# LayerNorms that start inside the last MLP block, two token tiles at a time

## The chip, the cores and the metric

The kernel runs on one core of one Trainium2 chip. The metric is device time in microseconds (us) of one execution of the whole program; smaller is better. The kernel before takes 2342.94 us (median of three runs, 2338.77 to 2347.87).

## The reference

A decoder trunk of two layers works on 1024 tokens of width 1024, all in float32. Each layer is a mixer, a LayerNorm, an MLP and a second LayerNorm:

```python
for layer in range(DEPTH):                      # DEPTH = 2
    if layer % 2 == 0:
        mix = hybrid_mixer(x, ...)              # sliding-window attention + gated DeltaNet, output projection
    else:
        mix = recurrent_mixer(x, ...)           # convolution, RG-LRU scan, gelu gate, output projection
    x = layer_norm(DN_ALPHA * x + mix, ln1_g[layer], ln1_b[layer])
    x = layer_norm(DN_ALPHA * x + sqrelu_mlp(x, mlp_w1[layer], mlp_w2[layer]), ln2_g[layer], ln2_b[layer])

def sqrelu_mlp(x, w1, w2):                      # w1: 1024 x 4096, w2: 4096 x 1024
    h = jax.nn.relu(x @ w1)
    return (h * h) @ w2
```

`layer_norm` takes mean and variance over the 1024 features of a token, scales by `rsqrt(var + 1e-5)`, multiplies by a gain and adds a bias.

## The kernel before

**Two streams.** The tokens are cut into two chunks of 512, chunk 0 and chunk 1 (`c` in the code). `stream(c)` is a generator that walks one chunk through the layers: `hybrid`, `mix_out` (output projection, residual, LayerNorm), `mlp_ln` (MLP, LayerNorm), four `rec_block`s, `mix_out`, `mlp_ln`. Chunk 1 needs states of chunk 0 in the mixers, so it runs behind. Each product is made of three float32r matmuls (`mm3`): an operand is split into a rounded high part and the rest (`wh`, `wl` for weights, `h`, `l` for activations), and high by high, high by low and low by high are summed in PSUM.

**The order of the work.** A loop at the end of `trunk` pulls the two streams in turn. `yield` is a point at which other work may be slipped in, `yield UNIT` ends a unit of about 24 matmuls, and `yield BLOCK` says that a stream cannot go on. Which stream goes next is set by a sort key: not the one marked shy, then the lower phase, then chunk 0. A stream is marked shy after a unit in which its flag `light[c]` is set, so a light stream alternates with the other one, unit by unit. Beside the streams there are mixers, small generators put in by `spawn` (the LayerNorms among them); one goes as soon as the time it asked for has come in a clock that the planner keeps of all engines. TensorE executes its instructions in exactly the order that comes out. The instructions of VectorE (DVE), ScalarE (ACT), GpSimd (POOL) and the DMA queues are ordered by a scheduler under the data dependencies.

**Shared tiles.** `g` is a pool of 14 tiles of 128x2048, `t`, `s` and `f` are rings of 11, 10 and 4 tiles of 128x512 (`RINGS`). PSUM has four banks for long sums (`mm`) and four for short work (`mx`). A weight block of 128x1024 is loaded into `ws` by SP's queue, and `split` makes `wh` (ACT, every fifth on DVE) and `wl` (DVE, some on POOL).

**The MLP.** `mlp` cuts the 4096 hidden features into 8 blocks of 512. `straight(e)` computes block `e` in the plain way: 4 x 24 matmuls with w1, then 4 x 24 with w2. Two blocks can also be done as a pair `j`: `first(j)` computes 8 x 24 matmuls with w1, and `seven(j)` does the w2 product of the pair with seven products in place of eight (Strassen's form), each of 24 matmuls, with sums of w2 quarters (`t1` to `t4`) that DMAs have made in DRAM. In `seven` DVE forms the differences, makes every `wl`, splits the operands and adds each result to y. `weave` runs `first(j+1)` and `seven(j)` side by side; for the last pair, `seven(3)`, there is no `first` left. In the last MLP of chunk 1, block 6 is done straight, and the last block is held back (`ends`, `finish`) so that the tail is short. y of a chunk lies in two `g` tiles, each with two token tiles of 128 tokens (`ytile(yg, n)`, n = 0 to 3).

**The LayerNorm.** `layernorm` first loads gain and bias into four tiles of the ring that its argument `r` names (`load_gb`, on ACT's queue). `coef(a, b)` turns the statistics of token tiles a to b-1 into mean, scale and offset with a chain of small DVE instructions, `norm(n, i)` normalizes half `i` of tile `n` (one ACT and two DVE instructions, or two on DVE), and, where a next stage needs x, four TensorE transposes per half go to an `mx` bank, from which `split_ps` writes `yT` (the four `g` tiles of `ActT`). With `yT` None the halves are stored to `out` by SP's queue.

In the kernel before a LayerNorm is spawned when its sum is complete: by `mix_out` after `out_proj`, by `mlp_ln` after `mlp`. For chunk 0 in layer 0 it is spawned only when chunk 1 has used up its own input of the MLP (`"m7" in sts[1]`), and four `g` tiles are free. Only in the last MLP of chunk 1 does it begin with the first finished token tile.

## Time and profile before

| | |
|---|---|
| median of three runs | 2342.94 us |
| the profiled execution, its own time | 2344.71 us |
| span of its instructions | 2342.9 us |
| mean granted TensorE clock | 0.983 |
| TensorE (PE) busy | 2237.1 us, 95% |
| VectorE (DVE) busy | 1552.0 us, 66% |
| ScalarE (ACT) busy | 1026.9 us, 44% |
| GpSimd (POOL) busy | 313.0 us, 13% |

Busy time of PE counts overlapping matmuls once. A product of 128x512 is listed with some 0.39 us, and starts about 0.227 us after the one before it when nothing holds it up, so the rate of a stretch is read from the number of its matmuls and not from its busy share. Stages can be found in the trace by the DRAM tensors that SP loads: chunk 0's mixer ends at about 354 us, chunk 1's at about 826 us; chunk 0's first MLP ends at about 971 us, chunk 1's at about 1360 us; the recurrent blocks of both chunks run from 1268 to about 1603 us, and the last MLP of chunk 0 ends at about 2001 us.

### The profile page before, as it was taken

What the parts mean: (1) busy time and instruction counts of PE and PEld (TensorE: products, weight loads), DVE (VectorE), ACT (ScalarE), POOL (GpSimd) and SP (SyncE); (2) the same over time, 40 slices, a digit from 0 to 9 for tenths busy, and PEclk for the clock granted to TensorE, in tenths of its full rate; (3) what the DMA queues carried; (4) which work ended last, traced back from release to release, by engine and by line L of the source; (5) the groups of instructions that cost most, each with busy time, mean ns of one, the idle gap of its engine ahead of it and who ended that gap; (6) DMA issues with size and microseconds to landing.
All of it is one profiled execution on the core that took longest, in us unless ns stands there. A gap on an engine that the chain in (4) does not pass through costs nothing.

```text
span 2342.9 us, 31999 instructions
## 1 busy us (share of the span) xinstructions
PE 2237.1 (95%) x12460; PEld 1799.1 (77%) x12460; DVE 1552.0 (66%) x2631; ACT 1026.9 (44%) x1759; POOL 313.0 (13%) x245
## 2 busy tenths in 40 slices
PE   8999997999999999899999979999999999999997
PEld 7676775677777887788887858777788887788886
DVE  6788759565664565766567877776635567745677
ACT  5364415443433134444344657655234444343452
POOL 3332313223321120000000000000110000100000
PEclk9999999999999999999999989999999999999999
DMA  4220231556676755767643333433233443434452
GB/s 156 65 77 31 78 126 63 135 162 191 174 220 196 196 167 172 238 201 219 214 142 126 126 126 105 161 99 129 100 97 121 135 153 126 145 108 152 144 172 72
DMA packets 86199, 329.07 MB, mean 140 GB/s; under 512 B 9504, under 2 KB 9888, under 8 KB 77856
## 3 DMA queue, kind: packets, MB, share of 16 engines
q1 hardware_dynamic: 72944, 272.17, 34.2%
q0 software_dynamic: 4608, 33.56, 7.6%
q10 hardware_dynamic: 8496, 21.30, 2.6%
q8 instruction: 98, 1.61, 0.3%
q14 instruction: 53, 0.43, 0.1%
HBM read 318.60 MB, written 75.50 MB: 168 GB/s over the span
## 4 chain that ended last, share of the span: by engine, by line
PE 76%; DVE 15%; ACT 3%; issue 2%; DMA 1%; POOL 0%; ACTq 0%; DVEq 0%; POOLq 0%
PE mm L206 61%; PE mx L206 14%; DVE g L178 6%; DVE s L178 2%; DVE wl L178 2%; DVE t L178 1%; DVE hsc L178 1%; PE mx L210 1%; DVE f L178 1%; ACT wh L178 1%; DVE lnw L178 1%; ACT s L178 1%; ACT t L178 1%; DMA ws<-t 0%; DVE lns L178 0%
## 5 line engine op out<-in xcount | busy, mean ns | idle before, releaser
L206 PE MATMUL mm<-g,wh 128*128 128x512 f32 x2816 | 886.1, 396 | 4.3 <-DVE g L178 4.3
L178 DVE TENSOR_TENSOR wl<-ws,wh 128x1024 fp32r<-128x1024 f32 (+1 forms) x377 | 460.9, 1223 | 361.7 <-ACT wh L178 358.3
L178 ACT CAST wh<-ws 128x1024 fp32r<-128x1024 f32 (+1 forms) x350 | 364.9, 1043 | 718.8 <-PE mm L206 656.3
L206 PEld LDWEIGHTS mm<-g,wh 128*128 128x128 f32 x2816 | 521.3, 189 | 112.6 <-DVE g L178 5.9
L206 PE MATMUL mm<-g,wl 128*128 128x512 f32 x1408 | 550.4, 391 | 0.0
L206 PE MATMUL mm<-wh,s 128*128 128x512 f32 x1280 | 423.2, 398 | 13.3 <-DVE g L178 8.6
L206 PEld LDWEIGHTS mm<-g,wl 128*128 128x128 f32 x1408 | 265.3, 188 | 56.6
L206 PEld LDWEIGHTS mm<-wh,s 128*128 128x128 f32 x1280 | 242.8, 190 | 68.8 <-ACT wh L178 6.4
L206 PE MATMUL mm<-wl,s 128*128 128x512 f32 x640 | 251.7, 393 | 1.4 <-DVE wl L178 1.4
L178 POOL TENSOR_TENSOR wl<-ws,wh 128x1024 fp32r<-128x1024 f32 (+1 forms) x61 | 150.5, 2467 | 728.9 <-ACT wh L178 389.5
L206 PE MATMUL mm<-wh,g 128*128 128x512 f32 (+1 forms) x768 | 231.6, 379 | 9.7 <-ACT wh L178 6.8
L206 PE MATMUL mx<-wh,s 128*128 128x512 f32 x528 | 171.7, 392 | 1.8 <-DVE s L178 1.8
L206 PEld LDWEIGHTS mm<-wh,g 128*128 128x128 f32 x768 | 142.4, 191 | 36.3 <-ACT wh L178 6.8
L206 PE MATMUL mm<-wl,g 128*128 128x512 f32 (+1 forms) x384 | 143.9, 375 | 0.3 <-DVE wl L178 0.3
L206 PEld LDWEIGHTS mm<-wl,s 128*128 128x128 f32 x640 | 121.4, 190 | 25.2 <-DVE wl L178 1.8
L178 ACT CAST s<-g 128x512 fp32r<-128x512 f32 x158 | 95.5, 623 | 99.7 <-PE mx L206 47.4
L178 DVE TENSOR_TENSOR s<-g,s 128x512 fp32r<-128x512 f32 x158 | 105.9, 686 | 42.3 <-ACT s L178 42.0
L206 PEld LDWEIGHTS mx<-wh,s 128*128 128x128 f32 x528 | 99.1, 188 | 23.1 <-DVE s L178 3.1
L178 DVE CAST wh<-ws 128x1024 fp32r<-128x1024 f32 x88 | 60.5, 687 | 80.3 <-PE mm L206 70.3
L178 DVE TENSOR_TENSOR g<-g,mm 128x512 f32<-128x512 f32 x140 | 92.6, 683 | 27.9 <-PE mm L206 27.5
L206 PE MATMUL mx<-wl,s 128*128 128x512 f32 x264 | 102.8, 389 | 0.0
L206 PEld LDWEIGHTS mm<-wl,g 128*128 128x128 f32 x384 | 73.2, 191 | 12.2 <-DVE wl L178 0.6
(235 smaller groups left out, 2607.3 us busy)
## 6 DMA issues: line engine op xcount, KB each, us to landing
ws<-w SPq DMA_DIRECT2D x234, 512.0 KB, 3.3
ws<-t SPq DMA_DIRECT2D x88, 512.0 KB, 3.3
t<-w POOLq DMA_DIRECT2D x32, 1024.0 KB, 8.6
ws<-hin_fm SPq DMA_DIRECT2D x32, 512.0 KB, 3.4
t<-w SPq DMA_DIRECT2D x16, 1024.0 KB, 7.9
t<-t SPq DMA_DIRECT2D x16, 1024.0 KB, 7.4
ws<-rin SPq DMA_DIRECT2D x32, 512.0 KB, 3.3
ws<-hout SPq DMA_DIRECT2D x16, 512.0 KB, 3.4
```

What stands on the lines that cost most here:

```text
L178: r = f(*a, **k)
L206: ins = self.pe.matmul(out, lhsT, rhs, start=start, stop=stop, skip_group_check=fresh)
L210: return self._pe(self.pe.transpose(out, x, ident), out, [x], 0.00042 * 2 * out.shape[-1])
```

## The change

A LayerNorm is now spawned before its sum is complete. `out_proj` and `mlp` get a dictionary with a function `start` and a count `n` of finished token tiles; `start` is called ahead of the second half of the output projection, ahead of the last straight block, or ahead of the last `seven`. `layernorm` waits for `n` twice: it makes coefficients and begins to normalize when two token tiles are there, and again for the other two. It still waits for the tiles of `yT` before its first transpose.

The flag `light[c]` is set while `seven` runs with no `first` beside it. Chunk 1's LayerNorm after the first MLP takes its gain and bias tiles from ring `s` in place of `t`. In the last MLP of chunk 1 block 6, the straight one, moves from the start to the place ahead of the last `seven`.

```diff
@@ layernorm
-            coef(0, NT)
-            norm(0, 0)
             for j, (n, i) in enumerate(halves):
-                if j + 1 < len(halves):
+                if j % 4 == 0:
+                    yield from wait(lambda: res.get("n", NT) >= n + 2)
+                    coef(n, n + 2)
+                    norm(n, i)
+                if j % 4 < 3:
                     norm(*halves[j + 1])
+                yield from wait(lambda: yT.g)
                 yield late(2.5, ytile(yg, n)[:, i * 512:(i + 1) * 512])
@@ mlp, straight
                 if half == 1:
                     free(ring, *(z for hl in own for z in hl))
+                    if done:
+                        res["n"] = NT
@@ mlp, seven
+                    if done and i in (4, 6) and p == 1:
+                        res["n"] = 2 + (i == 6) * 2
                     yield UNIT
@@ mlp, body
-        if res is not None:
-            yield from straight(6, False)
         while e < 8 and not (...):
+            if e == 7:
+                res["start"]()
             yield from straight(e, e == 7)
             e += 1
         if e < 8:
-            n = 3 if res is not None else 4
+            n = 3 if tail else 4
             yield from first(e // 2)
             for j in range(e // 2, n):
-                nxt = first(j + 1) if j + 1 < n else ends() if res is not None else None
+                nxt = first(j + 1) if j + 1 < n else ends() if tail else None
+                if j == n - 1:
+                    if tail:
+                        yield from straight(6, False)
+                    else:
+                        res["start"]()
+                light[c] = nxt is None
                 yield from weave(nxt, seven(j, hids.pop(j), j == 3), 2)
-        if res is not None:
+                light[c] = False
+        if tail:
             yield from finish()
@@ out_proj
         for half in range(2):
+            if half == 1:
+                res["start"]()
...
                 oT.free()
+                res["n"] = NT
@@ mix_out
+        s["yT"] = ActT()
+        f = dict(n=0, start=lambda: spawn(layernorm(s["yg"], ls, which, r, s["yT"], f)))
+        yield from out_proj(w, oT, resid, s["yg"], ls, f)
...
-        spawn(layernorm(s["yg"], ls, which, r, s["yT"], f))
@@ mlp_ln
-        f = dict()
+        f = dict(n=0, start=lambda: spawn(layernorm(s["yg"], ls, 2 * layer + 1, r, s["x"], f, each)))
...
+        yield from mlp(layer, c, s["yT"], s["yg"], ls, f, last and c == 1)
+        if not last:
+            if c == 0:
+                yield from wait(lambda: "m7" in sts[1])
+            yield from need("g", 4)
+            s["x"].claim()
@@ stream
-        yield from mlp_ln(0, c, s, "t", False)
+        yield from mlp_ln(0, c, s, "ts"[c], False)
```

The program has the same 10868 matmuls and transposes as before, and the same number of ACT instructions and of DMAs. DVE has 75 instructions more: 78 more of the small ones of `coef` (each now twice, on 2 columns where it had 4), and three `wl` fewer, which go to POOL. Three places show how the order moves.

**Place 1: SP's queue at the end of chunk 0's first MLP.** SP loads the weight blocks in the order in which TensorE uses them. `w1_0` is the first MLP weight, here for chunk 1's `first(0)`; `t1_0_3`, `t2_0_3`, `t3_0_3` and `t4_0_3` are sums of w2 for chunk 0's `seven(3)`, and so is `w2_0`. Before:

```order
L178 DMA ws_1212_8601<-t1_0_3_117 128x1024
L178 DMA t4_1_1_128<-t2_1_1_127 128x2048
L178 DMA ws_1217_8623<-t1_0_3_117 128x1024
L178 DMA ws_1222_8648<-t2_0_3_119 128x1024
L178 DMA ws_1227_8670<-t2_0_3_119 128x1024
L178 DMA ws_1232_8696<-w2_0 128x1024
L178 DMA ws_1237_8718<-w2_0 128x1024
L178 DMA ws_1242_8745<-t3_0_3_118 128x1024
```

And now:

```order
L178 DMA ws_1213_8630<-w1_0 128x1024
L178 DMA ws_1221_8670<-t1_0_3_117 128x1024
L178 DMA ws_1224_8688<-w1_0 128x1024
L178 DMA t1_1_2_129<-w2_1 128x2048
L178 DMA ws_1230_8726<-t1_0_3_117 128x1024
L178 DMA ws_1233_8746<-w1_0 128x1024
L178 DMA ws_1239_8784<-t2_0_3_119 128x1024
L178 DMA ws_1242_8802<-w1_0 128x1024
```

Before, the products of `seven(3)` stood alone; now a w1 block (24 matmuls) stands between every two halves of a product (12 matmuls each).

**Place 2: TensorE at the end of chunk 1's first MLP.** `g_1043` and `g_1044` are the two y tiles of chunk 1, and `mx<-csb,g` are the transposes of the LayerNorm, four for each half of a token tile; the other rows are chunk 0's third recurrent block. Before:

```order
L206 MATMUL mx_1825_11903<-g_1621_10880,wh_1823_11899 128x512
L206 MATMUL mx_1825_11903<-g_1620_10879,wl_1824_11900 128x512
L210 MATMUL mx_1831_11964<-csb_75,g_1043_7515 128x128 x4
L210 MATMUL mx_1832_11974<-csb_75,g_1043_7515 128x128 x4
L210 MATMUL mx_1833_11985<-csb_75,g_1043_7515 128x128 x4
L210 MATMUL mx_1834_11995<-csb_75,g_1043_7515 128x128 x4
L210 MATMUL mx_1835_12006<-csb_75,g_1044_7516 128x128 x4
L210 MATMUL mx_1836_12016<-csb_75,g_1044_7516 128x128 x4
L206 MATMUL mx_1841_12034<-g_1618_10877,wh_1839_12030 128x512
```

And now, where `g_1044_7529` is the y tile of token tiles 2 and 3:

```order
L206 MATMUL mx_1830_11972<-g_1623_10933,wl_1829_11969 128x512
L210 MATMUL mx_1831_11976<-csb_75,g_1043_7528 128x128 x4
L210 MATMUL mx_1832_11986<-csb_75,g_1043_7528 128x128 x4
L206 MATMUL mx_1830_11972<-g_1623_10933,wh_1828_11968 128x512
...
L210 MATMUL mx_1833_12009<-csb_75,g_1043_7528 128x128 x4
L210 MATMUL mx_1834_12016<-csb_75,g_1043_7528 128x128 x4
...
L210 MATMUL mx_1875_12230<-csb_75,g_1044_7529 128x128 x4
```

Before, six groups of transposes stood in a row behind 24 matmuls of the block. Now the transposes of tiles 0 and 1 stand in two pairs among the first 24 matmuls after the MLP, and those of tiles 2 and 3 come 88 rows later (the first) to 157 rows later (the last).

**Place 3: SP's queue at the end of chunk 0's last MLP.** `w1_1` belongs to chunk 1's `first(0)` (before: to its `straight(6)`), the others to chunk 0's `seven(3)`; `out` are stores of chunk 0's result. Before:

```order
L178 DMA ws_2617_16447<-t4_1_3_136 128x1024
L178 DMA ws_2622_16469<-t4_1_3_136 128x1024
L178 DMA ws_2625_16491<-w1_1 128x1024
L178 DMA ws_2635_16607<-w1_1 128x1024
L178 DMA ws_2640_16643<-w1_1 128x1024
L178 DMA ws_2649_16683<-w2_1 128x1024
L178 DMA out<-g_1992_12845 128x512 x2
```

And now:

```order
L178 DMA ws_2638_16764<-w1_1 128x1024
L178 DMA ws_2644_16801<-t3_1_3_134 128x1024
L178 DMA ws_2651_16829<-w2_1 128x1024
L178 DMA ws_2656_16851<-t4_1_3_136 128x1024
L178 DMA ws_2661_16873<-w2_1 128x1024
L178 DMA out<-g_1932_12597 128x512 x2
L178 DMA ws_2666_16897<-t4_1_3_136 128x1024
```

Here too w1 blocks now stand between the products of `seven(3)`, and the first stores have moved ahead of its last weight block.

## The prediction

> **What bounds the kernel now.** I read the page first, then busy times by stretch, then the chain of waits and the instructions in order of time where TensorE stands still.

> ```profile
> PE 2237.1 (95%) x12460; PEld 1799.1 (77%) x12460; DVE 1552.0 (66%) x2631; ACT 1026.9 (44%) x1759; POOL 313.0 (13%) x245
> PE 76%; DVE 15%; ACT 3%; issue 2%; DMA 1%; POOL 0%; ACTq 0%; DVEq 0%; POOLq 0%
> ```

> TensorE is the bound, and 15% of the chain that ends last is DVE. The change leaves TensorE's instructions as they are, so it can only take away, or add, time in which TensorE waits. I need the rate when nothing holds it up. From the chain in order of time (start, length, engine, count), and from the instructions in order of time:

> ```profile
> 1020.57 16.32 PE mm L206 x72
> 913.89 1.04 PE L210 MATMUL mx<-csb,g 128*128 128x128 f32 x8
> ```

> 16.32/72 = 0.227 us for a 128x512 matmul and 1.04/8 = 0.13 us for a transpose. Now the stretches around the LayerNorms (bounds in us, length, then busy us and count of PE, PEld, DVE, ACT, POOL, then granted clock, DMA share and GB/s):

> ```profile
> 913.20:927.00 13.80, 12.75 (x70) 9.67 (x68) 12.74 (x18) 10.09 (x18) 1.19 (x1) 1.00 0.48 158
> 927.00:950.00 23.00, 22.41 (x99) 18.30 (x98) 22.77 (x29) 11.38 (x16) 0.35 (x1) 1.00 0.78 242
> 950.00:971.40 21.40, 15.42 (x59) 12.26 (x59) 13.07 (x19) 4.41 (x5) 0.46 (x1) 0.84 0.62 179
> 1015.00:1060.00 45.00, 45.00 (x200) 37.28 (x199) 29.44 (x35) 20.89 (x28) 0.82 (x1) 1.00 0.71 219
> ...
> 1268.10:1366.20 98.10, 95.83 (x422) 78.69 (x421) 81.74 (x110) 60.38 (x85) 7.96 (x14) 1.00 0.38 124
> 1371.60:1383.60 12.00, 0.18 (x1) 0.00 (x0) 8.64 (x23) 8.05 (x13) 0.00 (x0) 0.61 0.55 173
> 1383.60:1400.40 16.80, 13.38 (x57) 10.51 (x58) 13.32 (x23) 6.55 (x11) 0.00 (x0) 0.67 0.31 125
> 1400.40:1492.60 92.20, 89.32 (x385) 72.79 (x384) 71.71 (x95) 71.82 (x104) 9.03 (x12) 0.98 0.43 146
> ...
> 1536.20:1603.40 67.20, 62.40 (x274) 49.91 (x273) 56.97 (x96) 47.67 (x71) 4.71 (x3) 0.95 0.38 126
> ...
> 1955.60:2001.70 46.10, 39.85 (x158) 31.08 (x157) 39.84 (x71) 19.82 (x26) 2.88 (x1) 0.93 0.42 136
> 2041.10:2090.10 49.00, 49.00 (x218) 40.56 (x217) 16.50 (x18) 20.34 (x29) 0.00 (x0) 1.00 0.29 97
> ```

> A loss is the length less 0.227 us for each matmul and 0.13 us for each of the 32 transposes of a LayerNorm.
> - Place 1, chunk 0's first `seven(3)` with nothing beside it: 13.8 - 12.8, 23.0 - 22.4 and 21.4 - 13.4, together 9.6 us. From 927 to 950 DVE is busy for 22.77 of 23.0 us: `seven` alone feeds DVE as much as TensorE.
> - Place 2, chunk 1's LayerNorm after its first MLP: 12.0 with TensorE idle, 16.8 - (25 x 0.227 + 32 x 0.13 = 9.8) = 7.0, and 92.2 - 87.3 = 4.9, together 23.9 us. The 98.1 us before it, in which `seven(3)` and recurrent blocks alternate, lose 2.4.
> - Place 3, chunk 0's LayerNorm among chunk 1's recurrent blocks: 67.2 - (242 x 0.227 + 4.2 = 59.1) = 8.1 us.
> - Place 4, chunk 0's last `seven(3)`: 46.1 - 35.8 = 10.3 us.

> The stretch from 1015 us, where w1 blocks and `seven` alternate, loses nothing with DVE at 29.44 of 45.0 us; nor does the one from 2041, w1 blocks alone.

> What is late in place 1 and 2 stands in the chain of waits and in DVE's instructions (start, length; in brackets its idle time and what ended that):

> ```profile
> 949.93 10.58 DMA ws<-t
> 1376.21 4.70 DMA t<-ln
> ...
> 1368.66 0.69 DVE L178 BATCH_NORM_STATS2 lns<-g 128x6 f32<-128x512 f32 x1
> 1377.66 0.17 DVE L178 SCALAR_TENSOR_TENSOR lnw<-lnw 128x4 f32<-128x4 f32 x1
> 1380.93 0.75 DVE L178 SCALAR_TENSOR_TENSOR g<-g,lnw,t 128x512 f32<-128x512 f32 x1 [3.10 <-DMA t<-ln]
> 1383.52 6.11 DVE L178 TENSOR_TENSOR g<-g,t 128x512 f32<-128x512 f32 x10
> ```

> In place 2 the last statistics end at 1369.4, the coefficients at 1377.8 (their small instructions stand between others), and then DVE waits 3.1 us for gain and bias, which could not be loaded before ring `t` gave up tiles to chunk 0's recurrent blocks; the first transposes follow at 1383.6.

> **The change part by part.**

> *Gain and bias from ring `s`, an early start, two tiles at a time (place 2).* The load is out of the way, so at least the 3.1 us go. Token tiles 0 and 1 are complete after the fifth of seven products, and their coefficients and norms fall in the stretch from 1268 to 1366, where DVE has 16.4 us to spare; half a LayerNorm is 6 `TENSOR_TENSOR` and 2 `SCALAR_TENSOR_TENSOR` of some 0.7 us and a chain of 13 small ones of 0.17, about 8 us. That fits, barely, so I add 2 us of loss there. TensorE's order now holds the transposes of tiles 2 and 3 back by 88 to 157 rows, at least 88 x 0.227 = 20 us, against the 14 us from last statistics to first transposes now; without the hole the clock does not fall either. I keep 6 of 23.9 us, gain 18. Bounds: 3 (the load alone) and 22.

> The clock row bears on this: 0.61 granted in the hole, 0.67 in the 16.8 us behind it, where 7.0 us are lost with DVE busy for 13.32. [...]

> *`light` during the last `seven` (places 1 and 4).* The order shows 24 w1 matmuls between halves of 12: 36 x 0.227 = 8.2 us of TensorE, for which DVE makes two `wl`, one operand split, one addition to y and its share of differences. From the groups (busy us, mean ns, idle before):

> ```profile
> L178 DVE TENSOR_TENSOR wl<-ws,wh 128x1024 fp32r<-128x1024 f32 x15 | 18.3, 1218 | 8.2 <-ACT wh L178 8.1
> L178 DVE TENSOR_TENSOR s<-g,s 128x512 fp32r<-128x512 f32 x13 | 8.7, 682 | 0.3 <-ACT s L178 0.3
> L178 DVE TENSOR_TENSOR g<-g,mm 128x512 f32<-128x512 f32 x8 | 5.2, 681 | 0.0
> ```

> 2 x 1.22 + 0.68 + 0.68 + some 0.6 = 4.4 of 8.2 us, a share like that of the stretch from 1015. The 10.58 us load of place 1 then has w1 work ahead of it. The LayerNorm's transposes at 913 to 927 stay where they were (1.0 lost), and the last two products alternate with products of the other chunk's first `seven`, which DVE hardly keeps up with. I keep 1.6 of 9.6 and 2.3 of 10.3: gain 8 each. Bounds 0 and 9.6, 0 and 10.3; no row speaks for a loss, since only independent work comes in between.

> In place 4 the stores of token tile 0 stand in SP's queue ahead of the last weight block of `seven(3)`. Whatever is behind a late store waits. Tiles 0 and 1 are complete two products earlier, with w1 between them: 2 x 2 x 8.2 = 33 us less the alternating end, against 8 us of LayerNorm work. I count nothing; a late store would cost up to those 8.

> *The moved LayerNorm in place 3.* The spawn before the second half of `out_proj` brings only the load ahead, since both halves of the features are needed. The order puts this LayerNorm, as before, among recurrent blocks of chunk 1, where DVE is busy for 56.97 of 67.2 us; w1 blocks come later. Gain 2 of 8.1; bounds -5 (two more recurrent blocks are now behind it, at the 4.9 us that their stretch from 1400 lost) and 8.

> *Block 6 straight, later.* It is TensorE work with a light DVE load wherever it stands; the row from 2041 shows w1 work at no loss, and its place at the start of chunk 1's MLP is taken by `first(0)`, also w1. Zero; if it left a hole, one product's 5.4 us.

> *The first LayerNorm, among chunk 1's mixer.* Here the order is only reshuffled, with the transposes some rows earlier:

> ```profile
> 354.70:450.00 95.30, 80.90 (x707) 56.66 (x706) 75.12 (x196) 49.20 (x124) 26.45 (x20) 0.95 0.32 94
> 378.46 4.45 DVE L178 TENSOR_TENSOR g<-g,s 128x512 f32<-128x512 f32 x2
> ```

> TensorE stands idle for 14.4 us of it, and two norms took 4.45 us together, with POOL at work. Zero, from -8 to 8 (half of those 14.4 us either way, rounded up).

> *78 more small instructions.* At 0.17 us that is 13 us of DVE in six LayerNorms, which counts only where TensorE waits for DVE: in the first one and in places 2 and 3, three of six. Half of their 6.5 us fall between other instructions: 3 us lost; bounds 0 and 13.

> Sum: 18 + 8 + 8 + 2 + 0 - 3 = 33 us. The profiled execution took 2344.71 us, 1.8 above the median, so the changed kernel comes to 2311.7 in such an execution and to **2310 us** in the median.

> **The rivals.**
> - *DVE is late next.* With the load gone, norms and transposes of the second half wait behind recurrent work on DVE (81.74 of 98.1 busy before it, and it now takes 8 us more). Then place 2 gains 8, place 3 loses 1, places 1 and 4 gain 6 each: 8 - 1 + 12 - 3 = 16, 2327 us. For it speaks how full DVE is, against it the 88 rows. 13%.
> - *A shorter hole that still drops the clock.* If 4 of the 12 us remain in place 2, the 7.0 behind them stay as well, and the 4.9: the gain there is 8 in place of 18, 2320 us. 12%. [...]
> - *Loads hide the alternation.* At a DMA share of 0.78 a block took 10.58 us; the w1 blocks stand in the same queue, behind it. Places 1 and 4 gain 1 each: 33 - 14 = 19, 2324 us. Against it speaks the row from 1015, no loss at 0.71. 6%.
> - *Slower: DVE's queue in chunk 1's mixer.* The reshuffled first LayerNorm puts both coefficient chains and norms ahead of the attention and DeltaNet chains that TensorE waits for. One whole LayerNorm (16 us of DVE, two halves of 8) late at each of four heads is 64 us against 33: 2374 us. It decides from 45 us more of TensorE idle between 354 and 783. Only 14.4 of the first 95.3 us are idle there now. 4%.
> - *Not what it says:* the early start is held by `g` or ring tiles and nothing moves, 2343. The order of the engines shows it moving: 2%.

> **How the numbers follow.** My forecast has 63%, with its own range 2298 to 2321 (its unknown costs, most of them place 2 and the mixer). The range that holds 8 of 10 reaches to the second and third rival: 2298 to 2329. This measurement tells about 0.5% from no change, 11.7 us: faster means below 2331.2. All of the forecast, nearly all of the clock and load rivals and two thirds of the first lie there: 0.88. Within 0.5%: 0.08. Slower: 0.04.

> **What would show it.** Right: no TensorE idle of 10 us after chunk 1's first MLP, and a granted clock near 1.00 there; the two lone `seven(3)` run at 0.227 us per matmul. Wrong: DVE above 95% with TensorE waiting for `g` in place 2; waits for `wh` or for SP's queue in places 1 and 4; more idle time in chunk 1's mixer than now, above all.

## The result, and the profile after

The changed kernel takes 2314.1 us (median of four runs, 2311.93 to 2316.76) beside 2344.59 us for the kernel before; the ratio is 0.9873, with a 95% interval from 0.985 to 0.9896. Its profiled execution took 2313.61 us, with a span of 2311.8 us and a mean granted clock of 0.988. From the page of the changed kernel, the busy times and the chain of waits:

```profile
PE 2226.8 (96%) x12460; PEld 1795.1 (78%) x12460; DVE 1552.7 (67%) x2706; ACT 1026.1 (44%) x1759; POOL 313.6 (14%) x248
PE 78%; DVE 13%; ACT 3%; issue 2%; POOL 0%; DMA 0%; DVEq 0%; ACTq 0%; POOLq 0%
```

The program has 10866 matmuls and transposes, not 10868; the page counts 12460, 1594 more, and 1594 is the number of its f32 products that are not transposes: each of these stands there twice. DVE's part of the chain went from 15 to 13%, TensorE's from 76 to 78%. The stretches that answer to those of the prediction (bounds in us, length, then busy us and count of PE, PEld, DVE, ACT, POOL, then granted clock, DMA share and GB/s):

```profile
918.60:932.40 13.80, 12.75 (x70) 9.66 (x68) 12.75 (x18) 10.09 (x18) 0.00 (x0) 1.00 0.36 122
932.40:955.00 22.60, 22.01 (x98) 17.94 (x96) 16.39 (x20) 8.45 (x13) 0.81 (x1) 1.00 0.77 233
955.00:976.40 21.40, 21.40 (x96) 17.73 (x95) 11.88 (x13) 9.76 (x13) 0.81 (x1) 1.00 0.68 200
...
1361.70:1434.60 72.90, 69.66 (x321) 57.18 (x321) 66.13 (x105) 57.04 (x83) 8.62 (x13) 1.00 0.43 144
...
1478.20:1531.50 53.30, 45.01 (x201) 36.33 (x200) 47.46 (x95) 41.26 (x61) 5.40 (x3) 0.90 0.21 69
1934.60:1980.70 46.10, 45.51 (x201) 37.40 (x200) 27.32 (x32) 18.22 (x25) 0.00 (x0) 1.00 0.37 128
354.20:450.00 95.80, 82.69 (x677) 58.30 (x677) 69.93 (x189) 46.63 (x110) 28.02 (x21) 0.89 0.33 95
```

The first three rows are place 1, now with w1 blocks between: behind the LayerNorm's transposes TensorE is idle for 0.6 of 44.0 us, and DVE has fallen from 22.77 of 23.0 us to 16.39 of 22.6. The fourth is place 2. It keeps a granted clock of 1.00, where the kernel before had 0.61 and 0.67, and loses 72.9 us less 69.5 (the rate of the prediction), 3.4 us. The fifth is place 3 with a clock of 0.90 and 11.0 us lost, 8.3 of them idle. The sixth is place 4, now at its rate. The last is the start of chunk 1's mixer, where the clock is 0.89; before, the same stretch had 0.95.

At the ends of all the stretches below TensorE has done the same number of instructions in both kernels, and up to the end of E also the same work, so the time from one to the next can be compared directly. (At the end of F the changed kernel has done other blocks in part, since block 6 comes later there; they are matmuls of the same shape.) The four columns are start to start in us in four profiled executions: the first traces of the two kernels, and a second one of each from the runs below.

| stretch of TensorE's order | before | before, second | changed | changed, second |
|---|---|---|---|---|
| up to chunk 1's mixer | 347.9 | 347.0 | 347.9 | 346.3 |
| A: chunk 1's mixer, with the first LayerNorm | 558.5 | 558.4 | 564.4 | 564.3 |
| B: place 1 and chunk 1's first MLP | 335.7 | 329.8 | 327.6 | 327.6 |
| C: chunk 1's `seven(3)` with recurrent blocks | 117.3 | 117.3 | 115.6 | 115.6 |
| D: places 2 and 3 | 370.0 | 369.2 | 351.2 | 351.2 |
| E: chunk 0's last MLP up to place 4 | 201.3 | 201.3 | 201.3 | 201.3 |
| F: place 4 | 152.6 | 152.6 | 143.6 | 143.6 |
| G: the rest | 239.6 | 239.6 | 240.6 | 240.6 |

A row repeats within 1 us, apart from the first (1.6 us) and from B in the kernel before. The change takes 18 to 19 us out of D, 9.0 out of F, 1.7 out of C, and 2.2 or 8.1 out of B, and it puts 5.9 into A and 1.0 into G. Together the rows differ by 31 us in the first traces and by 25 in the second.

### The profile page after: what moved, and what is told of

Read it like the earlier page. It is cut to its first block, busy times and chain, and to the rows that moved or that the text cites. A ratio compares the mean times of both kernels' runs of the same rounds, so it can differ in the third digit from the quotient of the medians.

```text
span 2311.8 us, 32057 instructions
## 1 busy us (share of the span) xinstructions
PE 2226.8 (96%) x12460; PEld 1795.1 (78%) x12460; DVE 1552.7 (67%) x2706; ACT 1026.1 (44%) x1759; POOL 313.6 (14%) x248
## 4 chain that ended last, share of the span: by engine, by line
PE 78%; DVE 13%; ACT 3%; issue 2%; POOL 0%; DMA 0%; DVEq 0%; ACTq 0%; POOLq 0%
PE mm L206 61%; PE mx L206 16%; DVE g L178 5%; DVE t L178 2%; DVE s L178 2%; DVE hsc L178 2%; DVE wl L178 1%; PE mx L210 1%; DVE f L178 1%; ACT wh L178 1%; ACT g L178 1%; ACT t L178 1%; ACT s L178 1%; ACT f L178 0%; ACT L178 0%
## 5 line engine op out<-in xcount | busy, mean ns | idle before, releaser
L206 PE MATMUL mm<-g,wh 128*128 128x512 f32 x2816 | 890.1, 397 | 2.7 <-DVE g L178 2.6
L178 DVE TENSOR_TENSOR wl<-ws,wh 128x1024 fp32r<-128x1024 f32 (+1 forms) x374 | 456.8, 1222 | 340.0 <-ACT wh L178 336.7
L178 ACT CAST wh<-ws 128x1024 fp32r<-128x1024 f32 (+1 forms) x350 | 365.1, 1043 | 719.9 <-PE mm L206 620.6
L206 PEld LDWEIGHTS mm<-g,wh 128*128 128x128 f32 x2816 | 522.2, 189 | 111.3 <-DVE g L178 3.9
L206 PE MATMUL mm<-g,wl 128*128 128x512 f32 x1408 | 551.8, 392 | 0.0
L206 PE MATMUL mm<-wh,s 128*128 128x512 f32 x1152 | 379.8, 395 | 3.6 <-DVE g L178 3.3
L206 PEld LDWEIGHTS mm<-g,wl 128*128 128x128 f32 x1408 | 266.0, 189 | 57.0
L178 POOL TENSOR_TENSOR wl<-ws,wh 128x1024 fp32r<-128x1024 f32 (+1 forms) x64 | 157.2, 2457 | 1010.1 <-ACT wh L178 861.4
L206 PEld LDWEIGHTS mm<-wh,s 128*128 128x128 f32 x1152 | 216.2, 188 | 51.1 <-DVE g L178 3.9
L206 PE MATMUL mm<-wh,g 128*128 128x512 f32 (+1 forms) x768 | 231.4, 379 | 9.3 <-ACT wh L178 6.4
L206 PE MATMUL mm<-wl,s 128*128 128x512 f32 x576 | 224.6, 390 | 0.0
L206 PE MATMUL mx<-wh,s 128*128 128x512 f32 x528 | 172.7, 392 | 1.8 <-DVE s L178 1.8
L206 PEld LDWEIGHTS mm<-wh,g 128*128 128x128 f32 x768 | 142.3, 190 | 35.9 <-ACT wh L178 6.4
L206 PE MATMUL mm<-wl,g 128*128 128x512 f32 (+1 forms) x384 | 143.8, 375 | 0.3 <-DVE wl L178 0.3
L178 ACT CAST s<-g 128x512 fp32r<-128x512 f32 x158 | 96.4, 623 | 100.3 <-PE mm L206 51.2
L178 DVE TENSOR_TENSOR s<-g,s 128x512 fp32r<-128x512 f32 x158 | 106.8, 687 | 38.7 <-ACT s L178 38.5
L206 PEld LDWEIGHTS mm<-wl,s 128*128 128x128 f32 x576 | 108.3, 188 | 20.6 <-DVE wl L178 0.3
L206 PEld LDWEIGHTS mx<-wh,s 128*128 128x128 f32 x528 | 99.1, 188 | 23.2 <-DVE s L178 3.1
L178 DVE CAST wh<-ws 128x1024 fp32r<-128x1024 f32 x88 | 62.7, 712 | 78.1 <-PE mm L206 68.4
L178 DVE TENSOR_TENSOR g<-g,mm 128x512 f32<-128x512 f32 x144 | 95.0, 683 | 20.0 <-PE mm L206 19.5
L206 PE MATMUL mx<-wl,s 128*128 128x512 f32 x264 | 102.8, 389 | 0.0
L206 PEld LDWEIGHTS mm<-wl,g 128*128 128x128 f32 x384 | 73.2, 191 | 12.2 <-DVE wl L178 0.6
```

The source lines that it names most:

```text
L178: r = f(*a, **k)
L206: ins = self.pe.matmul(out, lhsT, rhs, start=start, stop=stop, skip_group_check=fresh)
```

## The experiments

The theory to begin with was the prediction's sum: terms that stand each for itself. So the first runs did single edits alone on the kernel before, or took single edits out of the changed kernel. Stretches are named by the letters above.

**`light` alone.** On the kernel before:

```diff
+                light[c] = nxt is None
                 yield from weave(nxt, seven(j, hids.pop(j), j == 3), 2)
+                light[c] = False
```

> The kernel before with one edit of the change alone: light is set during the last seven product, so that it alternates with w1 work. Theory A (the prediction's steps are separate terms): places 1 and 4 gain 8.1 and 8.9 us, everything else stays, 2344.7 - 17 = 2327.7 us in a profiled execution; the losses of about 9.6 and 10.3 us there fall to 1 to 2, and the 12.0 us hole of place 2 stays as it is. Rival B (the alternation needs the early LayerNorm to have something to alternate with, or is hidden behind the 10.58 us load): 2340 to 2345 us.

Measured: 2364.71 us, a ratio of 1.0116 (1.0098 to 1.0134), so slower by 27 us, which neither theory had. B took 330.0 us, like the second trace of before: nothing gained in place 1. F took 177.0 in place of 152.6. From the busy times by stretch of this run, and from ACT's instructions in order of time (start, length; in brackets its idle time and what ended that):

```profile
1966.00:2004.00 38.00, 28.43 (x96) 20.81 (x96) 16.31 (x20) 11.36 (x17) 2.39 (x1) 0.87 0.22 74
1969.20:1972.60 3.40, 3.40 (x9) 2.65 (x9) 0.00 (x0) 0.00 (x0) 0.00 (x0) 0.50 0.31 117
1982.90:1986.30 3.40, 3.40 (x9) 2.62 (x9) 2.64 (x3) 0.00 (x0) 0.00 (x0) 0.50 0.10 42
1996.50:1999.90 3.40, 3.40 (x9) 2.62 (x9) 0.00 (x0) 0.00 (x0) 0.00 (x0) 0.51 0.16 66
```

```profile
1973.12 1.06 ACT L178 CAST wh<-ws 128x1024 fp32r<-128x1024 f32 x1 [5.04 <-PE mx L206]
1978.38 1.04 ACT L178 CAST wh<-ws 128x1024 fp32r<-128x1024 f32 x1 [4.20 <-PE mm L206]
1979.33 0.59 ACT L178 ACTIVATE r<-mm 128x512 f32<-128x512 f32 x1
1979.95 0.63 ACT L178 ACTIVATE r<-r 128x512 f32<-128x512 f32 x1
1980.61 0.62 ACT L178 CAST s<-r 128x512 fp32r<-128x512 f32 x1
1981.13 0.61 ACT L178 CAST s<-g 128x512 fp32r<-128x512 f32 x1
```

In 38.0 us TensorE starts 96 matmuls, 21.8 us of work, with DVE busy for 16.31 us only. Of the 16.2 us lost TensorE is idle for 9.6. The rest is lost while it is busy, most of it in three stretches of 3.4 us behind the waits, with a granted clock of 0.50 to 0.51 and 9 matmuls in each, 2.0 us of work (over the 38.0 us the granted clock is 0.87). What is late is an operand. The half of a product that comes next needs `s<-g`, and ACT makes it as the last of a row: it waits for the w1 block of `straight(6)` to end (`r<-mm`), squares, converts that block's own operand (`s<-r`), and only then converts the one that TensorE waits for. That takes place at three w1 blocks in a row, each time with a wait of 2.5 to 3.3 us. ACT's queue of this kernel, in order (the operands of `seven(3)` are `s_16223` and `s_16288`):

```
L178 ACTIVATE r_16218<-mm_16193 128x512
L178 ACTIVATE r_16218<-r_16218 128x512
L178 CAST s_16179<-r_16218 128x512
L178 CAST s_16223<-g_15399 128x512
L178 CAST wh_16312<-ws_16310 128x1024
L178 ACTIVATE r_16280<-mm_16255 128x512
L178 ACTIVATE r_16280<-r_16280 128x512
L178 CAST s_16181<-r_16280 128x512
L178 CAST s_16288<-g_15399 128x512
```

In the changed kernel the same place reads so, with the operands of the two halves of `t1` (`s_16363`, `s_16418`) and the two before them one behind the other, well ahead of any wait for a w1 block:

```
L178 CAST s_16146<-g_15494 128x512
L178 CAST s_16227<-g_15493 128x512
L178 CAST g_16091<-mx_16139 128x4x128
L178 CAST s_16301<-g_15493 128x512
L178 CAST s_16363<-g_15493 128x512
L178 CAST s_16418<-g_15493 128x512
```

The code gives a reason: `straight` takes 8 tiles of one ring, with `s` first, and ring `s` has 10. `seven` also looks in `s` first and finds two, one pair, which cannot be filled again before its matmuls are done; `first` takes no ring tiles. Where the tiles lie in the built programs agrees. From the second half of `t1` to the end of `t4`, all nine half products of this kernel take their operands from one and the same pair of the ten places of ring `s`; in the kernel before they go round four pairs, in the changed kernel five.

The pair can be seen at work where nothing alternates any more. `straight(6)` cannot begin its w2 products while `seven` holds banks for long sums (`kept`), so behind the third w1 block the last four products of `seven(3)` stand alone, as in the kernel before. Yet they take 36.9 us here and 27.2 there, and each conversion starts only when TensorE is done with the half product before it:

```profile
2004.20 0.62 ACT L178 CAST s<-g 128x512 fp32r<-128x512 f32 x1 [3.34 <-PE mm L206]
2008.27 0.62 ACT L178 CAST s<-g 128x512 fp32r<-128x512 f32 x1 [2.50 <-PE mx L206]
```

**Block 6 at the start again.** On the changed kernel, to test this:

```diff
+        if tail:
+            yield from straight(6, False)
         while e < 8 and not (...):
...
                 if j == n - 1:
-                    if tail:
-                        yield from straight(6, False)
-                    else:
+                    if not tail:
                         res["start"]()
```

> The changed kernel with the six straight products of block 6 back at the start of chunk 1's last MLP. TensorE's order at chunk 0's last seven(3) is then that of the kernel before with light alone, which lost 24 us there. Theory A (formed after that run: block 6's w1 products write operands that hold 8 of the small ring's tiles until its w2 products, so seven has one pair of operand tiles and no look-ahead, and each half of 12 waits for ACT and DVE behind the w1 products beside it): place 4 takes 170 to 178 us in place of 143.6, about 2313.6 + 30 = 2344 us. Rival B (the prediction's: block 6 is light work wherever it stands, zero; what light alone lost came from the late LayerNorm there): 2312 to 2317 us.

Measured: 2346.98 us, a ratio of 1.0022 (1.0013 to 1.0032) to the kernel before. F, where TensorE's order is now that of `light` alone, took 179.3 us in place of 143.6 (a little above theory A's 170 to 178), all other stretches were those of the changed kernel within 1 us. Without the move of block 6 the whole change is worth nothing; with it, 34 us less (2312.94 in the same comparison). That block 6 beside `seven(3)` is what costs, once `light` makes the two alternate, is shown twice. That it does so through the tiles of ring `s` and ACT's queue is read from the programs and the trace above; no run changed the ring's size alone. The four cases of F (the lower row is from the changed kernel with and without `light`, the latter in the next run):

| F, us | without `light` | with `light` |
|---|---|---|
| block 6 at the start | 152.6 | 177.0 and 179.3 |
| block 6 ahead of the last `seven` | 146.5 | 143.6 |

**The changed kernel without `light`.**

```diff
-                light[c] = nxt is None
```

> The changed kernel without light during the last seven product. Theory A (separate terms): places 1 and 4 lose 8.1 and 8.9 us again, 2313.6 + 17 = 2330.6 us. Rival B (with the early start the last two products have nothing to gain from alternating, since the gain of places 1 and 4 came from the LayerNorm that begins under them): 2314 to 2318 us.

Measured: 2322.44 us, a ratio of 0.9937 (0.9923 to 0.9952). B took 332.8 and F 146.5 us. So `light` is worth 5.2 us (from one trace) and 2.9 us here, together 8.1 of the 17 us that theory A had. Of the 9.0 us that the change takes out of F, 6.1 come without it, with block 6 gone from there and the LayerNorm begun earlier. No run separates the two, but 5.3 us of loss are gone at one place, where the first w1 block of block 6 and a half product behind it stood; this speaks for block 6 (the place is shown further down, in the part on why the prediction was right).

**The kernel before, once more.** No edit.

> The kernel before once more, word for word. The kernel with the ring alone has the same work in place 1 and loses less there: 329.8 us from the w1 block to the next stretch, where the trace of before has 335.7. Theory A (the 10.58 us load of place 1 was late by chance in that one trace, and the change gains only some 2 us there): place 1 takes 329 to 331 us here, the other stretches are within 1 us of the first trace, profiled execution 2338 to 2341. Theory B (the load is late in every execution of before, and the ring moved it): 335 to 336, 2343 to 2346.

Measured: 2342.58 us, a ratio of 1.0002; the profiled execution took 2336.9 us and B 329.8. The prediction quoted a load of 10.58 us there, the third of three `ws<-t` blocks in a row. The same block in the first trace (issued at 949.93 us) and in this one (issued at 948.78), with its size and the time to landing:

```profile
ws<-t SPq DMA_DIRECT2D x1, 512.0 KB, 10.6
ws<-t SPq DMA_DIRECT2D x1, 512.0 KB, 6.0
```

And the last third of place 1, which had 59 matmuls in 21.4 us in the first trace:

```profile
948.80:970.20 21.40, 19.36 (x86) 15.73 (x85) 17.24 (x30) 5.92 (x7) 0.81 (x1) 1.00 0.80 244
```

The load takes 6.0 us and not 10.6, and place 1 loses 5.9 us less, as theory A had it. The late load belongs to an execution, not to the kernel. Of the 14 traces of this study one other, that of four tiles at once, has a load of over 10 us in place 1 (10.8 us). The executions of the kernel before lie between 2336.9 and 2349.1 us here, those of the changed one in its second comparison between 2312.3 and 2314.6.

**The ring alone.** On the kernel before:

```diff
-        yield from mlp_ln(0, c, s, "t", False)
+        yield from mlp_ln(0, c, s, "ts"[c], False)
```

> The kernel before with one edit alone: chunk 1's LayerNorm after its first MLP loads gain and bias through ring s in place of ring t. Theory A (as the prediction's lower bound: the load alone is worth the 3.1 us for which DVE waited, the coefficients and norms still come after the last statistics, so a hole of about 9 us and the slow clock behind it stay): 2341.6 us, gain 3. Rival B (the load was the whole of it: with it out of the way the other chunk's recurrent work fills the hole, the hole falls below 3 us and the clock does not drop): gain 15 to 18 in place 2, about 2328 us. Rival C (the hole shrinks to some 4 us and the 7.0 us of slow clock behind it stay): gain 8, 2337 us.

Measured: 2330.93 us, a ratio of 0.9965 (0.9953 to 0.9977). D took 359.7 us, 9.5 less than in the second trace of before. It is nearest to rival C. Place 2 in this run:

```profile
1366.00:1380.00 14.00, 9.33 (x35) 7.00 (x34) 13.79 (x27) 13.66 (x21) 0.00 (x0) 0.83 0.41 150
1371.80:1375.20 3.40, 1.43 (x6) 0.82 (x5) 3.37 (x6) 3.40 (x6) 0.00 (x0) 1.00 0.32 130
1375.20:1382.00 6.80, 5.64 (x15) 4.55 (x16) 6.80 (x13) 6.80 (x12) 0.00 (x0) 0.50 0.52 208
```

The hole of 12 us is now one of 1.5 and one of 3.1 us, both ahead of products of chunk 0's recurrent block, with DVE busy nearly all the time, and the clock still halves for 6.8 us behind them.

**Two tiles at a time, with ring `t`.** On the changed kernel, the ring edit taken back:

```diff
-        yield from mlp_ln(0, c, s, "ts"[c], False)
+        yield from mlp_ln(0, c, s, "t", False)
```

> The changed kernel with gain and bias of chunk 1's LayerNorm after its first MLP loaded through ring t again. Theory A (the early start needs the ring: ring t gives up tiles to chunk 0's recurrent blocks only behind them, so the LayerNorm cannot begin early and the 12 us hole with the slow clock behind it comes back): place 2 and 3 lose 12 to 20 us, 2326 to 2334 us. Rival B (two tiles at a time carries place 2, the planner finds room for ring t): within 4 us of the changed kernel, 2310 to 2318 us.

Measured: 2329.94 us, a ratio of 0.9945 (0.9928 to 0.9962), C 129.8 and D 353.2 us, together 16.2 us more than in the changed kernel. The size is theory A's, the place is not. The LayerNorm does begin early, but with four tiles of ring `t` in its hands, and chunk 0's recurrent blocks work in that ring: after three of their units of 24 matmuls TensorE's order has the last four products of `seven(3)` with nothing between, and then 24 transposes in a row. Around these transposes, busy times by stretch:

```profile
1306.00:1335.00 29.00, 16.13 (x68) 11.90 (x68) 25.43 (x62) 12.29 (x17) 0.00 (x0) 0.76 0.43 154
```

In ring `s` the load stands in nobody's way: TensorE has recurrent blocks between.

**All four tiles at once.** On the changed kernel, load and spawn as they are:

```diff
-                if j % 4 == 0:
-                    yield from wait(lambda: res.get("n", NT) >= n + 2)
-                    coef(n, n + 2)
+                if j == 0:
+                    yield from wait(lambda: res.get("n", NT) >= NT)
+                    coef(0, NT)
                     norm(n, i)
-                if j % 4 < 3:
+                if j + 1 < len(halves):
```

> The changed kernel, but each such LayerNorm begins its coefficients only when all four token tiles are complete, once for four tiles; load and ring stay as changed. Theory A (the two-tile early start carries most of the 18.7 us of place 2): place 2 loses 15 us more, chunk 1's mixer 3 us less with 78 small instructions fewer, 2313.6 + 12 = 2326 us. Rival B (the ring carries place 2, the two-tile step only adds small instructions): place 2 stays within 3 us, the stretch from 354 to 913 us is 3 to 6 us shorter, 2308 to 2311 us.

Measured: 2317.57 us, a ratio of 0.9916 (0.9901 to 0.993), between the two. D took 357.4 us, 6.2 more than the changed kernel; A took 559.9, 4.5 less. C and D together tell what carries place 2:

| kernel | C + D, us | gained |
|---|---|---|
| before, second trace | 486.5 | |
| the changed kernel with ring `t` | 483.0 | 3.5 |
| ring `s` alone | 477.0 | 9.5 |
| early spawn and ring `s`, four tiles at once | 473.0 | 13.5 |
| changed: ring `s`, two tiles | 466.8 | 19.7 |

3.5 (all of the change but the ring) and 9.5 (the ring) do not add up to 19.7: each edit makes room for the other.

**The changed kernel once more, and two kernels for stretch A.** The first has no edit. The second spawns the LayerNorms after the two `out_proj` at the old place; the third does that too and gives them four tiles at once.

```diff
-            if half == 1:
-                res["start"]()
...
         s["ln0"]["ln0"] = True
+        f["start"]()
```

```diff
+        m = NT if which % 2 == 0 else 2
...
-                if j % 4 == 0:
-                    yield from wait(lambda: res.get("n", NT) >= n + 2)
-                    coef(n, n + 2)
+                if j % (2 * m) == 0:
+                    yield from wait(lambda: res.get("n", NT) >= n + m)
+                    coef(n, n + m)
                     norm(n, i)
-                if j % 4 < 3:
+                if j % (2 * m) < 2 * m - 1:
```

> The changed kernel once more, word for word, so that its stretches stand beside those of the experiments on one chip. All theories: 2310 to 2317 us; place 1 (913 to 1249 us before) within 3 us of 327.6, chunk 1's mixer (354 to 913) within 2 of 564.4. If place 1 or the mixer differ by more, their differences between single traces are of that size too and a term that rests on one of them is no firmer.

> The changed kernel, but the LayerNorms after the two out_proj are spawned where they were before the change, after the claim of the tiles; two token tiles at a time stays. Theory A (what chunk 1's mixer lost, 5.9 us, comes from the early spawn, which puts load and norms at another place among its work): mixer 558 to 560 us, 2308 to 2310 us. Rival B (it comes from the second chain of 13 small instructions that DVE must do before the second half): mixer stays at 563 to 565, 2313 us.

> As the run before it, and those LayerNorms also take all four token tiles at once; only the LayerNorms after an MLP keep two at a time. Theory A (early spawn): nothing more than 1 us better than the run before it in chunk 1's mixer. Rival B (small instructions): mixer 558 to 560 us in place of 564, and place 3 (chunk 0's LayerNorm among recurrent blocks, 11.0 us lost) 2 to 3 us better, so about 2305 to 2308 us. Against both, the planner puts the transposes of place 3 one by one from 24 rows earlier on, which may give back some us there.

Measured: 2312.94 us for the changed kernel, a ratio of 0.988 (0.9863 to 0.9896); 2311.76 with the late spawn (0.9875, 0.9858 to 0.9891); 2314.45 with four tiles too (0.9882, 0.986 to 0.9903). A took 564.3, 564.0 and 561.9 us. So the early spawn costs A nothing, and the two steps of the first LayerNorm cost it some us. The third kernel gives that back in D, 355.0 in place of 351.2, where the planner has put the transposes of place 3 in other places.

**Four tiles for the first LayerNorm only.** So the next kernel keeps all of the change but for that one LayerNorm: the last diff without the late spawn, and with

```diff
+        m = NT if which == 0 else 2
```

> The changed kernel, but the first LayerNorm of each chunk takes all four token tiles at once; all others stay at two. TensorE's order after chunk 1's mixer is that of the changed kernel. Theory A (what the mixer lost is two holes that fill over half of a 3.41 us window each, at 363 and 394 us, in which the second coefficient chain stands in DVE's queue, so that the clock is halved for 3.4 and 10.2 us in place of once for 10.2): one slow stretch of 10.2 us is left between 354 and 450, the mixer takes 559 to 562 us in place of 564.4, 2309 to 2311 us. Rival B (the mixer's loss comes from the rest of the changed order): 564, 2313 us.

Measured: 2310.01 us (2305.53 to 2311.4), a ratio of 0.9856 (0.9838 to 0.9875). A took 558.9 us, as in the kernel before. What the two steps did to A, in busy times by stretch, first of the changed kernel and then of this one:

```profile
363.40:366.80 3.40, 1.47 (x8) 0.83 (x7) 3.40 (x21) 2.22 (x3) 0.67 (x3) 1.00 0.00 0
366.80:370.20 3.40, 3.40 (x11) 2.81 (x11) 3.40 (x10) 1.02 (x2) 0.00 (x0) 0.50 0.00 0
...
394.10:397.50 3.40, 1.30 (x10) 0.82 (x8) 3.30 (x6) 3.40 (x8) 1.30 (x2) 1.00 0.37 141
397.50:407.80 10.30, 8.22 (x51) 5.04 (x51) 7.18 (x14) 1.71 (x4) 4.34 (x3) 0.50 0.40 121
```

```profile
363.40:366.80 3.40, 2.50 (x19) 1.95 (x17) 3.40 (x15) 3.29 (x5) 0.00 (x0) 1.00 0.00 0
...
394.10:397.50 3.40, 2.83 (x47) 1.81 (x46) 3.26 (x6) 3.05 (x6) 1.63 (x2) 1.00 0.32 102
397.50:407.80 10.30, 8.64 (x85) 4.87 (x85) 8.47 (x18) 4.13 (x8) 3.05 (x3) 1.00 0.32 121
```

The holes themselves are short: in the first row TensorE is idle for 1.9 us of 3.4. But the clock halves behind them, for 3.4 and for 10.2 us; with one step the same stretches keep 1.00. Between 354 and 450 us the clock is halved for 20.5 us in the changed kernel, and for 10.2 in this one and in the kernel before. This kernel has the lowest median of the study, but its interval overlaps that of the changed kernel (0.9863 to 0.9896), so it is not shown to be faster; in the traces the spans are 2308.5 beside 2311.8 and 2310.4 us. What is shown is the direction in A. TensorE's order in A is the same in all kernels with two steps there, and with one step it is that of the kernel before. The six traces with two steps have A at 563.4 to 564.5 us, the eight with one step at 556.7 to 562.2.

**And `light` during the second `out_proj`.** On that kernel, in `stream`:

```diff
-        light[c] = False
         yield from mix_out(I["rout"], ...)
+        light[c] = False
```

> As the run before it, and light stays set for chunk 0 during its second out_proj, so that it alternates with recurrent blocks of chunk 1 and the LayerNorm of place 3 begins later among other blocks. Theory A (place 3 loses 11.0 us because DVE is full there, and more TensorE work ahead of its transposes fills part of the 5.9 and 2.6 us holes): place 3 gains 3 to 6 us, 2305 to 2308 us. Rival B (DVE has the same work for the same TensorE work, so the hole only moves): within 2 us of the run before it. Rival C (its transposes stand singly between products now, and each waits): 2 to 5 us slower than the run before it.

Measured: 2310.83 us (0.986, 0.984 to 0.988). D took 353.5 beside 351.5 us: the holes of place 3 moved and did not go (rival B). A took 562.2 us beside 558.9, though TensorE's order there is the same; the last section tells why.

## Why the prediction was right, and where it was not

**The sum.** 33 us were forecast and 2310 us; it came to 28 to 30 us by the ratios, 2313 to 2314 us. The time is within the likeliest case's own range. The terms are less good than their sum, and that the sum came near is in part luck, as the terms of place 4 and block 6 show.

**Place 2, gain 18.** Its loss fell from 23.9 to 3.4 us, and the 2 us of loss that I added for the stretch before it were a gain of 1.7 (C). The step held: no idle of 10 us is left, the clock stays at 1.00, and DVE is full (66.13 of 72.9 us) but makes TensorE wait for 2.0 us only. My lower bound, 3 us for the load alone, was too low: the ring alone gave 9.5, because gain and bias in time let the planner move the transposes too.

**`light` in places 1 and 4, gain 8 each.** This is the step that failed, in its size and in its ground. In place 1 I sized the loss from one execution with a late load; the second trace has 5.9 us less, and the gain left is 2.2 us. (I also put that load beside a DMA share of 0.78; it was issued at 949.93 us, and the row in which it ran has 0.62.) In place 4 the 9.0 us came, but only 2.9 of them by `light`. And "no row speaks for a loss, since only independent work comes in between" is wrong. The work was independent, but ACT's queue and the ring were shared, and `light` alone cost 24 us in F. A row of the kernel before already spoke for it. There one w1 block of block 6 stands between two halves of a product, from 1955.60 us, and the half behind it waits for its operand:

```profile
1964.48 0.57 PE L206 MATMUL mm<-wh,s 128*128 128x512 f32 x1 [3.28 <-ACT s L178]
```

The block and the half lose 5.3 us together, half of the 10.3 us of place 4, which the prediction treated like place 1, as time lost to DVE. (What it says of a late store in SP's queue is in that trace too: a store that had waited 4.2 us for DVE goes out at 2007.40 us and takes 0.34, and the weight load behind it follows at 2007.84, without a wait of its own.) `light` on the kernel before made three more such places. In the changed kernel without `light` the w1 block there is one of `first(0)`, and neither it nor the half behind it loses anything.

**Block 6, zero.** Wrong by 34 us in the changed kernel, where `light` is set. I looked at what block 6 does to DVE and at w1 work at no loss in the row from 2041, but that work is `first`, which takes no operand tiles. The two wrong steps cancel in the changed kernel, since there block 6 is out of the way when `light` sets in. In place 4 the gain came out near the forecast for a reason that the prediction did not have.

**Place 3, gain 2.** It lost 2.9 us more, 11.0 in place of 8.1, within the bounds. DVE is at 47.46 of 53.3 us, and the holes are at its norms; TensorE's instructions in order of time:

```profile
1512.17 1.11 PE L210 MATMUL mx<-csb,g 128*128 128x128 f32 x4 [5.69 <-DVE g L178]
1515.53 1.22 PE L206 MATMUL mx<-s,wh 128*128 128x512 f32 x2 [2.24 <-DVE g L178]
```

**The first LayerNorm 0, small instructions 3.** Stretch A lost 5.9 us more, within the bounds of -8 to 8. The two steps were the right thing to cost, the price was not that of the instructions, 0.17 us each. It was what the clock does behind the short holes that come with the two steps: one step for that LayerNorm gave back 5.5 us in that trace, and between 1.2 and 7.8 us over all traces with one and with two. Whether the second chain itself or the order that comes with it makes the holes was not separated.

**The rivals.** The slower one, in chunk 1's mixer, named a place that did lose, at a tenth of its price; 45 us of idle time were far off. A shorter hole that still drops the clock did not come in place 2, but it is what the ring alone shows there, with holes of 1.5 and 3.1 us and 6.8 us at half clock, and what A shows, with 1.9 us of idle time and 3.4 us at half clock. The 4 us that this rival left of the hole were an assumption. The case that would have made the change worthless, two streams whose operands share a queue and a ring, was not among the rivals.

## What to carry to other kernels

Work that is independent on the engine that sets the end can still meet in the queue of a helper engine and in the tiles of a ring, as `light` alone showed here at a price of 24 us: before two streams are made to alternate, look at which operands each holds and at the order of the conversions on the other engine's queue, and cost each edit with and without the others. Take a stall's size from more than one execution when a transfer ends it: the same load took 10.6 us in one and 6.0 in another. And count a small hole by what the clock does behind it, not by its own length: 1.9 us of idle time at 363 us had 3.4 us at half clock behind them.

## What was not expected of the hardware

| the window began at | busy share of it | before: windows, and followed by the other clock | changed | 14 traces |
|---|---|---|---|---|
| full clock | less than 45% | 7, 7 | 6, 6 | 105, 101 |
| full clock | 45 to 62% | 7, 3 | 6, 1 | 93, 18 |
| full clock | more | 643, 0 | 643, 0 | 9021, 0 |
| half clock | at least 80% | 12, 10 | 8, 7 | 127, 119 |
| half clock | less | 9, 0 | 6, 0 | 71, 0 |

The bounds of 45, 62 and 80% only sort these counts; no run shows where a limit lies. Not all windows that were followed by half clock were idle: 1.9 us of idle time did it at 363 us (a window 43% busy), while the hole of 1.84 us in place 2 of the changed kernel, of which 1.6 us lie in one window, 54% busy, did not:

```profile
1366.90:1370.30 3.40, 1.82 (x10) 1.61 (x11) 3.40 (x9) 2.26 (x4) 0.00 (x0) 1.00 0.51 154
1370.30:1373.70 3.40, 3.40 (x16) 2.79 (x16) 3.40 (x7) 1.06 (x1) 0.10 (x1) 1.00 0.00 0
```

The raster does not follow the program: the last two kernels have the same order on TensorE in stretch A and the same hole of 2.43 us near 485 us. In the one without `light` in `out_proj` the raster cuts the hole in two windows, 61 and 68% busy, and nothing follows:

```profile
482.80:486.20 3.40, 2.07 (x11) 1.46 (x10) 3.40 (x2) 1.04 (x1) 3.40 (x3) 1.00 0.00 0
486.20:489.60 3.40, 2.30 (x10) 1.93 (x11) 3.40 (x8) 0.40 (x2) 0.69 (x1) 1.00 0.79 219
```

In the other it lies in one window, 29% busy, and the next 3.4 us run at half clock:

```profile
484.30:487.70 3.40, 0.97 (x5) 0.49 (x4) 3.40 (x3) 1.04 (x1) 2.76 (x2) 1.00 0.15 28
487.70:491.10 3.40, 3.40 (x9) 2.63 (x9) 3.34 (x8) 0.40 (x2) 0.00 (x0) 0.50 1.06 273
```

With a second such pair, near 420 us, this makes A 3.3 us longer in the one execution than in the other. Differences of that size between single executions of kernels with holes of 2 us tell nothing about the kernels. Why some windows between 45 and 62% halve the clock and most do not stays open.
